# Expert weights in transfers of two chunks: five tiles of 16 KB per partition in a decoder layer on one Trainium2 core

## The chip, the cores and the metric

The kernel runs on one core of a Trainium2 chip. The metric is device time in microseconds (us), the median of three runs. The trace shown here is of one further, profiled execution of the kernel before.

## What is computed

One layer of a decoder on 256 tokens of width 1024 in float32. The last stage is a mixture of experts: each token goes to 2 of 32 experts.

```python
# Layer l:
#   h  = RMSNorm(x)
#   [u | v | q | k | vb] = h @ W_in
#   mixer A: y_a = u * (tril(W_s) RMSNorm(v) + b), chunks of 128
#   mixer B: differential attention with QK-norm and ALiBi
#   merged = sigmoid(h Wg_a) * (y_a Wup_a) + sigmoid(h Wg_b) * (y_b Wup_b)
#   x = x + merged @ W_out
#   x = x + HierMoE(RMSNorm(x))   (top-1 group, then top-2 experts inside the group)
def expert_block(args):
    tk, c = args
    hid = jax.nn.silu(jnp.einsum('td,edf->tef', tk, w1)) * jnp.einsum('td,edf->tef', tk, w3)
    hid = hid * c[:, :, None].astype(hid.dtype)
    return jnp.einsum('tef,efd->td', hid, w2)
```

The experts' weights w1, w3 and w2 are 96 MiB, two thirds of all that the kernel reads.

## The kernel before

**The stream of weights.** All weights reach the core as 136 chunks of 128 partitions x 8 KB (1 MiB): 40 chunks `wf` for the projections, then 96 chunks `wm` for the experts. `Stream` (line 98) sends them in a fixed order on SP's DMA queue. `pump` (line 106) issues the next chunk whenever the number of free slots is above a reserve. The kernel is written with a manual schedule, so the program text sets the order on every queue.

**The slots.** `Slots` (line 50) keeps a list of free buffers. There are 22 slots of 8 KB per partition: 3 are kept for the split projection weights (`hl`), 19 serve everything else: chunks, the activations `xT`, `xh`, `xl`, the mixers' results and so on. Two more are added when early pools close, and the 3 for `hl` join at the end of the projections. In the experts' stage two further slots come from the four-part gate tiles that are no longer needed; a chunk in such a slot is loaded by four transfers of 256 KB, with 2 KB per partition (line 121). A slot that is dropped goes to the end of the list, and `take_chunk` (line 73) takes the first of the list. In the program, the transfer into a slot waits for the last reader of what was there before. The DMA completions of one queue go round eight semaphores (`DMAHW0` to `DMAHW7`), so a transfer also waits until the one eight places before it has landed.

**The experts' stage.** The 32 experts are eight groups of four (`NGRP`). A group (`products`, line 1020) reads 12 chunks. Chunks 0 to 7 hold w1 and w3 for 128 input features each: matmuls of line 1025 into `h`. Then silu and product, two transposes (line 1039), and chunks 8 to 11 hold w2 for 256 output columns each: matmuls of line 1067 into `y`, which line 1046 adds to the tokens' result `res`. In between stand the next group's gathering (line 976). After each chunk `done_` (line 1119) drops the slot and pumps the stream:

```python
        def done_():
            slots.drop(box["w"])
            st.pump(0)
```

Chunk n of the experts is thus chunk n mod 12 of group n div 12. In the last group (`store`), dummy matmuls on a constant (line 215) follow each of the chunks 0 to 7, 20 of them each (30 after the last), and the output columns are copied and stored as soon as they are final.

If a token's expert overflows, a loop repeats the groups; `ci` holds the number of repetitions, 0 with these inputs. Each engine loads it once (line 1145).

Of the kernel before, what the change touches and what calls it, by code (L numbers as in the profile page):

```python
# [5 lines left out]
F32 = mybir.dt.float32  # L6
# [9 lines left out]
P = 128  # L16
# [25 lines left out]
NGRP = 8  # L42
NCH = 12
# [6 lines left out]
class Slots:  # L50


    def __init__(self, pool, tag, n):
        self.free = []
        self.owner = {}
        self.k = 0
        self.add(pool, tag, n)

    def add(self, pool, tag, n):
        self.free += [(pool, f"{tag}{i}") for i in range(n)]  # L60

    def add_pieces(self, pool, tags):
        self.free.append((pool, tags))

    def take(self, shape, dtype, name):
        i = [isinstance(tag, str) for _, tag in self.free].index(True)
        s = self.free.pop(i)
        self.k += 1
        t = s[0].tile(shape, dtype, tag=s[1], name=f"{name}_{self.k}")
# [3 lines left out]
    def take_chunk(self):

        if isinstance(self.free[0][1], str):
            return self.take([P, 2048], F32, "w")
        s = self.free.pop(0)
        self.k += 1
        t = tuple(s[0].tile([P, 512], F32, tag=tag, name=f"w_{self.k}_{i}") for i, tag in enumerate(s[1]))
        self.owner[id(t)] = (s, t)  # L80
        return t

# [15 lines left out]
class Stream:  # L98


    def __init__(self, nc, slots, srcs):
        self.nc, self.slots, self.srcs = nc, slots, srcs
        self.ready = []
        self.i = 0

    def pump(self, reserve):
        while self.i < len(self.srcs) and len(self.slots.free) > reserve:
            src = self.srcs[self.i]
            if self.i == len(self.srcs) - 1:
                if all(not isinstance(tag, str) for _, tag in self.slots.free):  # L110
                    break
                t = self.slots.take([P, 2048], F32, "w")
                c = 0
                for _, w in COLS[-1]:
                    self.nc.sync.dma_start(t[:, c * 8:(c + w) * 8], src[:, c * 8:(c + w) * 8])
                    c += w
            else:
                t = self.slots.take_chunk()
                if isinstance(t, tuple):
                    for e in range(4):  # L120
                        self.nc.sync.dma_start(t[e], src[:, e * 512:(e + 1) * 512])
                else:
                    self.nc.sync.dma_start(t, src)
            self.ready.append(t)
            self.i += 1

    def claim(self):

        t = self.slots.take([P, 2048], F32, "w")
        self.ready.append(t)  # L130
        self.i += 1
        return t
# [16 lines left out]
def body(tc, cp, sp, tp, mmp, axp, xT_d, xn_d, wf_d, wm_d, wst_d, bs_d, pv_d, rb_d, wr_d, out_d):  # L149
    nc = tc.nc  # L150
    V, S, G, TE = nc.vector, nc.scalar, nc.gpsimd, nc.tensor
    slots = Slots(sp, "s", NSLOT - 3)
    hl_slots = Slots(sp, "h", 3)
# [29 lines left out]

    stream = Stream(nc, slots, [wf_d[i] for i in range(40)] + [wm_d[g, c] for g in range(NGRP) for c in range(NCH)])
    pv = cp.tile([P, PV_N], F32, name="pv")
# [960 lines left out]
    with tc.If(more > 0):  # L1146
        with tc.For_i(0, more, 1):
            V.tensor_scalar(pos_m, pos_m, -float(SL), None, ALU.add)
            st = Stream(nc, slots, [wm_d[g, c] for g in range(NGRP) for c in range(NCH)])
            st.pump(0)  # L1150
# [8 lines left out]
def prep(i):  # L1159
# [27 lines left out]
    for _, n in COLS[-1]:  # L1187
# [11 lines left out]
        "wf": wf,  # L1199
        "wm": wm.reshape(NGRP, NCH, P, 2048),  # L1200
        "wst": A("w_s").transpose(2, 0, 1),
# [18 lines left out]
```

## Time and profile before

| quantity | value |
|---|---|
| median of 3 runs | 468.51 us (467.79 to 469.26) |
| profiled execution, its own time | 468.38 us |
| span of the profile | 466.7 us |
| PE busy | 438.9 us (94%) |
| DVE, ACT, POOL busy | 207.4, 175.3, 94.7 us |
| bytes by DMA | 148.80 MB, 319 GB/s over the span |
| transfers of 1 MiB from the experts' weights | 89, and 24 of 256 KB and 2 of 512 KB |

The span is 1.68 us shorter than the execution's own time. PE counts as busy while it runs matmuls, whether they are at full speed or not. The page cuts the span into 40 slices and shows each engine's busy share in tenths, the TensorE clock that was granted, and the GB/s that were moved. The chain of waits follows back from the last instruction what released each step. SP is the engine whose queue issues all weight transfers; a row "SPq" is such an issue.

### The profile page before, as it was taken

The page shows a single profiled execution, that of the slowest core. Times are in us where ns is not written, and L with a number is a line of the kernel's source. Part 1 is how long each engine was busy: PE and PEld are TensorE (multiplying, and loading weights), DVE is VectorE, ACT ScalarE, POOL GpSimd, SP SyncE. Part 2 cuts the span into 40 slices and gives each one's busy share as a digit, 9 for nine tenths or more (in the row PEclk, how much of TensorE's full clock was granted, in tenths as well). Part 3 has the DMA queues.
Part 4 walks back from the last instruction along what each step waited for, and adds up shares of the span by engine and source line. Part 5 has one row for each costly group of instructions (what it writes and reads, how often), then busy time and mean ns, then how long its engine had stood idle before and what let it go on. Part 6 is the DMA issues. An engine that isn't in the chain of part 4 may idle for free.

```text
span 466.7 us, 8463 instructions
## 1 busy us (share of the span) xinstructions
PE 438.9 (94%) x3446; PEld 334.8 (72%) x3446; DVE 207.4 (44%) x389; ACT 175.3 (38%) x332; POOL 94.7 (20%) x118
## 2 busy tenths in 40 slices
PE   8989999999999999999999996989898989889984
PEld 6768778878999999999998842645545554636542
DVE  4676576778797655555774643111111011110012
ACT  5747657665665655533444341111000010101001
POOL 1057296456568100004000100000000000000000
PEclk9999999999999999999999998999999999999998
DMA  7999992550227887598767889999999999999992
GB/s 244 344 425 421 416 402 105 180 179 2 93 91 268 322 312 271 213 364 302 310 239 303 315 326 407 422 418 421 406 418 420 421 418 413 412 421 419 422 382 88
DMA packets 27453, 148.80 MB, mean 319 GB/s; under 512 B 3216, under 2 KB 6032, under 8 KB 11152
## 3 DMA queue, kind: packets, MB, share of 16 engines
q1 hardware_dynamic: 27264, 148.18, 80.3%
q8 instruction: 29, 0.48, 0.4%
q14 instruction: 16, 0.13, 0.1%
q10 hardware_dynamic: 144, 0.02, 0.0%
HBM read 147.14 MB, written 1.05 MB: 318 GB/s over the span
## 4 chain that ended last, share of the span: by engine, by line
PE 81%; DMA 7%; DVE 3%; ACT 3%; issue 2%; POOL 1%; SPq 1%; ACTq 0%
PE h L1025 10%; PE y L1067 7%; PE gp L976 6%; PE res L1046 6%; DMA w<-in_wm_dram 4%; DMA xn<-in_xn_dram 2%; PE v L355 2%; PE u L384 2%; PE ga L386 2%; PE b L386 2%; PE b L385 2%; PE b L384 2%; PE a L386 2%; PE a L385 2%; PE a L384 2%
## 5 line engine op out<-in xcount | busy, mean ns | idle before, releaser
L343 DVE TENSOR_TENSOR hl<-w,hl 128x1024 fp32r<-128x1024 f32 (+2 forms) x88 | 90.8, 1036 | 63.3 <-ACT hl L339 61.0
L339 ACT CAST hl<-w 128x1024 fp32r<-128x1024 f32 (+1 forms) x88 | 84.6, 968 | 83.9 <-PE a L386 12.8
L1025 PE MATMUL h<-w,hT 128*32 128x512 f32 x512 | 61.6, 598 | 0.5 <-DMA w<-in_wm_dram 0.4
L984 DVE TENSOR_TENSOR hT<-gp,pv 128x512 f32<-128x512 f32 (+1 forms) x19 | 11.3, 606 | 98.5 <-PE gp L976 98.5
L345 POOL TENSOR_TENSOR hl<-w,hl 128x352 fp32r<-128x352 f32 x32 | 40.5, 1275 | 21.8 <-ACT hl L339 21.7
L1067 PE MATMUL y<-w,hidT 128*32 128x256 f32 (+1 forms) x528 | 34.1, 389 | 4.9 <-issue 4.4
L1073 ACT COPY yy<-y 128x256 f32<-128x256 f32 (+1 forms) x33 | 12.1, 366 | 69.7 <-PE y L1067 69.7
L976 PEld LDWEIGHTS gp<-Sg,acc 128*128 128x128 f32 x256 | 30.4, 192 | 9.2 <-issue 8.0
L1011 POOL TENSOR_TENSOR Sw<-Sg,C 128x128 f32<-128x128 f32 x16 | 6.1, 399 | 151.4 <-PE res L1046 137.0
L1046 PE MATMUL res<-yy,SwT 128*128 128x128 f32 (+1 forms) x192 | 34.8, 323 | 1.1 <-ACT yy L1073 1.0
L1046 PEld LDWEIGHTS res<-yy,SwT 128*128 128x128 f32 x192 | 25.9, 190 | 12.0 <-issue 6.4
L976 PE MATMUL gp<-Sg,acc 128*128 128x128 f32 x256 | 32.0, 278 | 2.1 <-DVE Sg L972 2.1
L1025 PEld LDWEIGHTS h<-w,hT 128*32 128x32 f32 x512 | 13.4, 109 | 24.6 <-issue 19.2
L1067 PEld LDWEIGHTS y<-w,hidT 128*32 128x32 f32 x528 | 16.1, 112 | 17.1 <-issue 9.7
L1035 ACT ACTIVATE hid<-h 128x256 f32<-128x256 f32 x8 | 3.1, 383 | 54.8 <-PE h L1025 54.8
L1036 DVE TENSOR_TENSOR hid<-hid,h 128x256 f32<-128x256 f32 x8 | 3.4, 421 | 35.1 <-ACT hid L1035 35.1
L215 PEld LDWEIGHTS <-ones_b 128*128 128x128 bf16 x205 | 13.2, 106 | 7.8 <-issue 6.7
L384 PE MATMUL u<-xh,hl 128*128 128x256 f32 x64 | 18.8, 293 | 0.0
L384 PE MATMUL ga<-xh,hl 128*128 128x256 f32 x64 | 18.2, 284 | 0.0
L386 PE MATMUL ga<-xh,hl 128*128 128x256 f32 x64 | 18.1, 283 | 0.0
L385 PE MATMUL ga<-xl,hl 128*128 128x256 f32 x64 | 18.1, 283 | 0.0
L384 PE MATMUL gb<-xh,hl 128*128 128x256 f32 x64 | 18.1, 283 | 0.0
(219 smaller groups left out, 957.3 us busy)
## 6 DMA issues: line engine op xcount, KB each, us to landing
w<-in_wm_dram SPq DMA_DIRECT2D x89, 1024.0 KB, 12.6
w<-in_wf_dram SPq DMA_DIRECT2D x36, 1024.0 KB, 11.6
w<-in_wm_dram SPq DMA_DIRECT2D x24, 256.0 KB, 9.1
w<-in_wf_dram SPq DMA_DIRECT2D x8, 256.0 KB, 4.9
w<-in_wf_dram SPq DMA_DIRECT2D x4, 512.0 KB, 8.2
xT<-in_xT_dram SPq DMA_DIRECT2D x8, 128.0 KB, 4.9
xn<-in_xn_dram SPq DMA_DIRECT2D x1, 1024.0 KB, 8.7
xs<-in_xn_dram SPq DMA_DIRECT2D x1, 1024.0 KB, 9.4
```

The source lines that it names most:

```text
L215: TE.matmul(wps[:, :P], ones_b, ones_b, start=True, stop=True)
L339: S.copy(hl[:, 0, c], raw[:, c])
L343: V.tensor_tensor(hl[:, 1, c.start:m], raw[:, c.start:m], hl[:, 0, c.start:m].bitcast(F32), ALU.subtract)
L345: G.tensor_tensor(hl[:, 1, m:c.stop], raw[:, m:c.stop], hl[:, 0, m:c.stop].bitcast(F32), ALU.subtract)
L384: TE.matmul(o, wh, ah[:, kc], start=kc == 0, stop=False)
L385: TE.matmul(o, wh, al[:, kc], start=False, stop=False)
L386: TE.matmul(o, wl, ah[:, kc], start=False, stop=kc == KC - 1)
L976: TE.matmul(ps[:, i * P:(i + 1) * P], h2[:, t, kc * P:(kc + 1) * P], st["S"][:, t].rearrange("p e s -> p (e s)"), start=start, stop=t == N ...
L1025: TE.matmul(ps[e * SL:(e + 1) * SL], st["h"][kc // 4][:, kc % 4, e * SL:(e + 1) * SL], piece(w, e), start=kc == 0, stop=kc == KC - 1)
L1046: TE.matmul(res[t][c // 512][:, c % 512:c % 512 + n], st["SwT"][:, t * P:(t + 1) * P], yy[:, o:o + n], start=False, stop=True, skip_group_ ...
L1067: TE.matmul(py[e * SL:(e + 1) * SL, :n], hidT[:, f, e * SL:(e + 1) * SL], w[e][:, f], start=f == 0, stop=f == 1)
L1073: S.copy(yy, py[:, :n])
```

## The change

Ten of the 19 slots are now the halves of five tiles of 16 KB per partition, named `sd0` to `sd4`; nine single slots stay. Chunks are ordered on the host so that chunks 2i and 2i+1 of the experts lie side by side, 16 KB per partition. Up to chunk 29 each chunk is loaded alone, into a half or gate parts if one is free, else into a single slot. From chunk 30 to chunk 93 `pump` issues one transfer of 2 MiB for two chunks; it needs a 16 KB tile with both halves free, and stops if there is none. The last two chunks are loaded alone again.

```diff
+NTWO = 5
+TWO = 30
...
-    def __init__(self, pool, tag, n):
+    def __init__(self, pool, tag, n, n2=0):
...
+        for i in range(n2):
+            t = pool.tile([P, 4096], F32, tag=f"{tag}d{i}", name=f"{tag}d{i}")
+            self.free += [("half", t, h) for h in range(2)]
...
+    def pop(self, *kinds):
+
+        for kind in kinds:
+            for s in self.free:
+                if s[0] in kind:
+                    self.free.remove(s)
+                    self.k += 1
+                    return s
+        return None
...
+    def take_two(self):
+
+        for s in self.free:
+            if s[0] == "half":
+                both = [(*s[:2], h) for h in range(2)]
+                if all(any(f[0] == "half" and f[1] is s[1] and f[2] == h for f in self.free) for h in range(2)):
+                    self.free = [f for f in self.free if f[0] != "half" or f[1] is not s[1]]
+                    return s[1], [self.own(x, s[1][:, h * 2048:(h + 1) * 2048]) for h, x in enumerate(both)]
+        return None
...
     def pump(self, reserve):
-        while self.i < len(self.srcs) and len(self.slots.free) > reserve:
+        n = len(self.srcs)
+        while self.i < n and len(self.slots.free) > reserve:
             src = self.srcs[self.i]
-            if self.i == len(self.srcs) - 1:
-                if all(not isinstance(tag, str) for _, tag in self.slots.free):
+            if self.i == n - 1:
+                t = self.slots.take_chunk(("half", "tile"))
+                if t is None:
                     break
...
+            elif self.two <= self.i < n - 2:
+                x = self.slots.take_two()
+                if x is None:
+                    break
+                self.nc.sync.dma_start(x[0], self.pairs[self.i])
+                self.ready += x[1]
+                self.i += 2
+                continue
             else:
-                t = self.slots.take_chunk()
+                t = self.slots.take_chunk(("half", "pieces"), ("tile",))
...
-    slots = Slots(sp, "s", NSLOT - 3)
+    slots = Slots(sp, "s", NSLOT - 3 - 2 * NTWO, NTWO)
...
-    stream = Stream(nc, slots, [wf_d[i] for i in range(40)] + [wm_d[g, c] for g in range(NGRP) for c in range(NCH)])
+    stream = Stream(nc, slots, [wf_d[i] for i in range(40)], wm_d, 40 + TWO)
...
-        "wm": wm.reshape(NGRP, NCH, P, 2048),
+        "wm": wm.reshape(NGRP, NCH // 2, 2, P, 2048).transpose(0, 1, 3, 2, 4).reshape(NGRP, NCH // 2, P, 4096),
```

The instructions of PE, ACT, DVE and POOL keep their order. SP's queue changes at three places. A number at a name's end counts allocations; `sd0_70` and so on are the five wide tiles, and a load of 128x2048 into one of them fills a half.

The first place is SP's queue where chunks 8 to 18 of the experts are loaded, one a row (before the change):

```order
L123 DMA w_63_2295<-in_wm_dram 128x2048 [waits DMAHW0_49,DVE_49]
L123 DMA w_64_2353<-in_wm_dram 128x2048 [waits DMAHW1_49,DVE_49]
L123 DMA w_65_2382<-in_wm_dram 128x2048 [waits DMAHW2_49,PE_49]
L123 DMA w_66_2384<-in_wm_dram 128x2048 [waits DMAHW3_49]
L123 DMA w_67_2415<-in_wm_dram 128x2048 [waits DMAHW4_49,DVE_49]
L123 DMA w_68_2480<-in_wm_dram 128x2048 [waits DMAHW5_49,DVE_49]
L123 DMA w_69_2549<-in_wm_dram 128x2048 [waits DMAHW6_49,DVE_49]
L123 DMA w_70_2618<-in_wm_dram 128x2048 [waits DMAHW7_49,DVE_49]
L123 DMA w_71_2653<-in_wm_dram 128x2048 [waits DMAHW0_49,PE_49]
L123 DMA w_72_2678<-in_wm_dram 128x2048 [waits DMAHW1_49]
L123 DMA w_73_2714<-in_wm_dram 128x2048 [waits DMAHW2_49,DVE_49]
```

and now:

```order
L163 DMA sd0_70<-in_wm_dram 128x2048 [waits DMAHW0_49,DVE_49]
L163 DMA sd0_70<-in_wm_dram 128x2048 [waits DMAHW1_49,DVE_49]
L163 DMA w_65_2345<-in_wm_dram 128x2048 [waits DMAHW2_49,PE_49]
L163 DMA w_66_2347<-in_wm_dram 128x2048 [waits DMAHW3_49]
L163 DMA w_67_2378<-in_wm_dram 128x2048 [waits DMAHW4_49,DVE_49]
L163 DMA sd1_71<-in_wm_dram 128x2048 [waits DMAHW5_49,DVE_49]
L163 DMA w_69_2511<-in_wm_dram 128x2048 [waits DMAHW6_49,DVE_49]
L163 DMA sd1_71<-in_wm_dram 128x2048 [waits DMAHW7_49,DVE_49]
L163 DMA w_71_2614<-in_wm_dram 128x2048 [waits DMAHW0_49,PE_49]
L163 DMA sd2_72<-in_wm_dram 128x2048 [waits DMAHW1_49,DVE_49]
L163 DMA sd2_72<-in_wm_dram 128x2048 [waits DMAHW2_49,DVE_49]
```

Before, each chunk had a slot of its own. Now these chunks lie in the wide tiles: `sd0` holds chunks 8 and 9, `sd1` chunks 13 and 15, `sd2` chunks 17 and 18.

The second place is SP's queue from the load of chunk 25 on. Before:

```order
L123 DMA w_81_2964<-in_wm_dram 128x2048 [waits DMAHW7_49,PE_49]
L123 DMA w_82_2973<-in_wm_dram 128x2048 [waits DMAHW0_49,PE_49]
L123 DMA w_83_2990<-in_wm_dram 128x2048 [waits DMAHW1_49,PE_49]
L123 DMA w_84_3034<-in_wm_dram 128x2048 [waits DMAHW2_49,PE_49]
L123 DMA w_85_3043<-in_wm_dram 128x2048 [waits DMAHW3_49,PE_49]
L123 DMA w_86_3052<-in_wm_dram 128x2048 [waits DMAHW4_49,PE_49]
L123 DMA w_87_3069<-in_wm_dram 128x2048 [waits DMAHW5_49,PE_49]
L123 DMA w_88_3080<-in_wm_dram 128x2048 [waits DMAHW6_49,PE_49]
L123 DMA w_89_3099<-in_wm_dram 128x2048 [waits DMAHW7_49,PE_49]
L123 DMA w_90_3112<-in_wm_dram 128x2048 [waits DMAHW0_49,PE_49]
```

and now:

```order
L163 DMA sd3_73<-in_wm_dram 128x2048 [waits DMAHW7_49,PE_49]
L163 DMA sd3_73<-in_wm_dram 128x2048 [waits DMAHW0_49,PE_49]
L163 DMA sd4_74<-in_wm_dram 128x2048 [waits DMAHW1_49,PE_49]
L163 DMA w_84_2990<-in_wm_dram 128x2048 [waits DMAHW2_49,PE_49]
L163 DMA w_85_2999<-in_wm_dram 128x2048 [waits DMAHW3_49,PE_49]
L1185 TENSOR_LOAD ci_2867 [waits DVE_49]
L1185 ISA x2
L153 DMA sd0_70<-in_wm_dram 128x4096 [waits DMAHW4_49,PE_49]
L153 DMA sd1_71<-in_wm_dram 128x4096 [waits DMAHW5_49,PE_49]
L153 DMA sd2_72<-in_wm_dram 128x4096 [waits DMAHW6_49,PE_49]
L153 DMA sd3_73<-in_wm_dram 128x4096 [waits DMAHW7_49,DMAHW0_49,PE_49]
L153 DMA sd4_74<-in_wm_dram 128x4096 [waits DMAHW1_49,PE_49]
```

Chunks 25, 26 and 27 now lie in `sd3`, `sd3` and `sd4`; the other half of `sd4` holds chunk 5. From chunk 30 on one transfer of 4096 elements per partition stands for two of 2048. Before, the sixth row (chunk 30) took the slot of chunk 5; now the first wide transfer goes to `sd0`, so it waits for PE to be done with chunks 8 and 9. The load of the repetition count has moved from the queue's end to a place ahead of the wide transfers.

The third place is the end of the stream on SP's queue. Before:

```order
L123 DMA w_147_3868<-in_wm_dram 128x2048 [waits DMAHW5_49,PE_49]
L123 DMA w_148_3874<-in_wm_dram 128x2048 [waits DMAHW6_49,PE_49]
L123 DMA w_149_3893<-in_wm_dram 128x2048 [waits DMAHW7_49,PE_49]
L123 DMA w_150_3906<-in_wm_dram 128x2048 [waits DMAHW0_49,PE_49]
L115 DMA w_151_3932<-in_wm_dram 128x1024 [waits DMAHW1_49,PE_49]
L115 DMA w_151_3932<-in_wm_dram 128x1024 [waits DMAHW2_49]
```

and now:

```order
L153 DMA sd4_74<-in_wm_dram 128x4096 [waits DMAHW4_49,PE_49]
L153 DMA sd0_70<-in_wm_dram 128x4096 [waits DMAHW5_49,PE_49]
L153 DMA sd1_71<-in_wm_dram 128x4096 [waits DMAHW6_49,PE_49]
L161 DMA w_86_0_3912<-in_wm_dram 128x512
L161 DMA w_86_1_3913<-in_wm_dram 128x512
L161 DMA w_86_2_3914<-in_wm_dram 128x512
L161 DMA w_86_3_3915<-in_wm_dram 128x512 [waits DMAHW7_49]
L147 DMA w_87_3920<-in_wm_dram 128x1024 [waits DMAHW0_49]
L147 DMA w_87_3920<-in_wm_dram 128x1024 [waits DMAHW1_49]
```

The wide transfers are 32, and each takes the tile that the one five places before it filled. Chunk 94 goes into gate parts and chunk 95 into a single slot, whose readers have long been done, so that only the tiles are waited for.

## Rows read from the trace of the kernel before

**Rows 1.** Page, busy time by engine and the 40 slices of GB/s.

```profile
PE 438.9 (94%) x3446; PEld 334.8 (72%) x3446; DVE 207.4 (44%) x389; ACT 175.3 (38%) x332; POOL 94.7 (20%) x118
...
GB/s 244 344 425 421 416 402 105 180 179 2 93 91 268 322 312 271 213 364 302 310 239 303 315 326 407 422 418 421 406 418 420 421 418 413 412 421 419 422 382 88
```

**Rows 2.** Windows: start:end length, busy by engine, PE clock, DMA share, GB/s.

```profile
280.00:290.00 10.00, 5.75 (x48) 2.73 (x44) 3.85 (x15) 2.32 (x6) 0.48 (x2) 0.96 0.99 404
290.00:300.00 10.00, 10.00 (x97) 6.43 (x94) 1.19 (x3) 1.49 (x4) 0.76 (x2) 0.87 1.01 423
310.00:320.00 10.00, 8.35 (x94) 5.40 (x90) 1.54 (x3) 1.50 (x4) 0.76 (x2) 1.00 1.02 424
```

**Rows 3.** Waits of SP's queue, 340 to 440 us: total, times, longest.

```profile
SPq L123 <- DMA w<-in_wm_dram: 63.1, 35, 3.0
...
SPq L123 <- PE h L1025: 0.4, 2, 0.2
```

**Rows 4.** Waits of PE's weight loads, 290 to 430 us.

```profile
PEld h L1025 <- DMA w<-in_wm_dram: 2.1, 7, 0.3
```

**Rows 5.** Timeline of PE, last group: start, us, line, operation, [idle before <- releaser].

```profile
430.17 1.06 PE L1025 MATMUL h<-w,hT 128*32 128x512 f32 x8
...
432.38 1.06 PE L1025 MATMUL h<-w,hT 128*32 128x512 f32 x8
...
446.64 1.07 PE L1025 MATMUL h<-w,hT 128*32 128x512 f32 x8 [0.19 <-DMA w<-in_wm_dram]
...
450.28 1.07 PE L1067 MATMUL y<-w,hidT 128*32 128x256 f32 x16 [0.56 <-issue]
...
458.22 0.65 PE L1067 MATMUL y<-w,hidT 128*32 128x128 f32 x16
```

**Rows 6.** Timeline of SP's queue, three narrow windows around single issues.

```profile
293.17 0.33 SPq L123 DMA_DIRECT2D w<-in_wm_dram  x1
...
305.12 0.59 SPq L123 DMA_DIRECT2D w<-in_wm_dram  x1
...
309.82 0.33 SPq L123 DMA_DIRECT2D w<-in_wm_dram  x1
```

**Rows 7.** Timeline of PE in groups 0 to 2.

```profile
289.85 3.25 PE L1067 MATMUL y<-w,hidT 128*32 128x256 f32 x32 [0.52 <-DVE hidT L1041]
...
303.14 3.64 PE L1025 MATMUL h<-w,hT 128*32 128x512 f32 x32
...
312.70 1.93 PE L1067 MATMUL y<-w,hidT 128*32 128x256 f32 x32 [0.63 <-issue]
...
322.46 1.92 PE L1025 MATMUL h<-w,hT 128*32 128x512 f32 x16
...
324.68 3.64 PE L1025 MATMUL h<-w,hT 128*32 128x512 f32 x32
...
344.00 1.49 PE L1025 MATMUL h<-w,hT 128*32 128x512 f32 x12
```

**Rows 8.** Transfers of `w`, issue to landing, window 180 to 256 us.

```profile
DMA to landing us min/median/max: 4.7/6.7/10.1
```

**Rows 9.** DMA: packets and mean rate, 410 to 430 us, then 393.2 to 394.8 us.

```profile
DMA packets 1153, 8.41 MB, mean 421 GB/s; under 512 B 127, under 2 KB 127, under 8 KB 127
...
q1 hardware_dynamic: 1151, 8.39, 101.0%
...
DMA packets 176, 0.68 MB, mean 425 GB/s; under 512 B 21, under 2 KB 21, under 8 KB 117
...
q1 hardware_dynamic: 176, 0.68, 107.1%
```

**Rows 10.** Timeline of DVE: the repetition count.

```profile
282.32 0.15 DVE L1139 CAST ci<-cs 128x1 int32<-128x1 f32 x1
```

**Rows 11.** Page, the two queues that load instructions: packets, MB, share of 16 engines.

```profile
q8 instruction: 29, 0.48, 0.4%
q14 instruction: 16, 0.13, 0.1%
```

More of the change, by code (lines that the diff above doesn't have):

```diff
@@ L57, in __init__ @@
         self.add(pool, tag, n)
+        for i in range(n2):
+            t = pool.tile([P, 4096], F32, tag=f"{tag}d{i}", name=f"{tag}d{i}")
+            self.free += [("half", t, h) for h in range(2)]
     def add(self, pool, tag, n):
-        self.free += [(pool, f"{tag}{i}") for i in range(n)]
+        self.free += [("tile", pool, f"{tag}{i}") for i in range(n)]
     def add_pieces(self, pool, tags):
[L63 to L69, printed above, removed]
+        self.free.append(("pieces", pool, tags))
@@ L70, in take, with own @@
+    def pop(self, *kinds):
[6 more added lines that the diff above has]
+        return None
+    def own(self, s, t):
         self.owner[id(t)] = (s, t)
         return t
[L73 to L81, printed above, removed]
+    def take(self, shape, dtype, name):
+        s = self.pop(("tile",))
+        return self.own(s, s[1].tile(shape, dtype, tag=s[2], name=f"{name}_{self.k}"))
@@ new lines, in take_chunk @@
+    def take_chunk(self, *kinds):
+        s = self.pop(*kinds)
+        if s is None:
+            return None
+        if s[0] == "half":
+            t = s[1][:, s[2] * 2048:(s[2] + 1) * 2048]
+        elif s[0] == "tile":
+            t = s[1].tile([P, 2048], F32, tag=s[2], name=f"w_{self.k}")
+        else:
+            t = tuple(s[1].tile([P, 512], F32, tag=tag, name=f"w_{self.k}_{i}") for i, tag in enumerate(s[2]))
+        return self.own(s, t)
+    def take_two(self):
+        for s in self.free:
+            if s[0] == "half":
+                both = [(*s[:2], h) for h in range(2)]
+                if all(any(f[0] == "half" and f[1] is s[1] and f[2] == h for f in self.free) for h in range(2)):
+                    self.free = [f for f in self.free if f[0] != "half" or f[1] is not s[1]]
+                    return s[1], [self.own(x, s[1][:, h * 2048:(h + 1) * 2048]) for h, x in enumerate(both)]
+        return None
@@ L98, with __init__ @@
 class Stream:
-    def __init__(self, nc, slots, srcs):
-        self.nc, self.slots, self.srcs = nc, slots, srcs
+    def __init__(self, nc, slots, wf, wm, two):
+        self.nc, self.slots, self.two = nc, slots, two
+        self.srcs = wf + [wm[g, c // 2][:, c % 2 * 2048:(c % 2 + 1) * 2048] for g in range(NGRP) for c in range(NCH)]
+        self.pairs = [None] * len(wf) + [wm[g, c // 2] for g in range(NGRP) for c in range(NCH)]
         self.ready = []
@@ L106, in pump @@
     def pump(self, reserve):
-        while self.i < len(self.srcs) and len(self.slots.free) > reserve:
+        n = len(self.srcs)
+        while self.i < n and len(self.slots.free) > reserve:
             src = self.srcs[self.i]
-            if self.i == len(self.srcs) - 1:
-                if all(not isinstance(tag, str) for _, tag in self.slots.free):
+            if self.i == n - 1:
+                t = self.slots.take_chunk(("half", "tile"))
+                if t is None:
                     break
-                t = self.slots.take([P, 2048], F32, "w")
                 c = 0
@@ L127, in claim @@
     def claim(self):
-        t = self.slots.take([P, 2048], F32, "w")
+        t = self.slots.take_chunk(("half",))
         self.ready.append(t)
@@ L1148, in body @@
             V.tensor_scalar(pos_m, pos_m, -float(SL), None, ALU.add)
-            st = Stream(nc, slots, [wm_d[g, c] for g in range(NGRP) for c in range(NCH)])
+            st = Stream(nc, slots, [], wm_d, 0)
             st.pump(0)
```

## The prediction

> **What bounds the kernel now.** I read the page first. PE is busy 94% of the span, but the bytes moved stand at 406 to 422 GB/s in each slice from the 25th to the 38th, that is from about 280 us to 443 us [rows 1]. So there are two candidates for the experts' stage, and the reader should look at who waits for whom.
>
> The queue that issues the weights waits, from 340 to 440 us, 63.1 us for earlier transfers to land and 0.4 us for matmuls of line 1025 to free a slot [rows 3]. So the stream is never short of slots there: the transfers stand back to back and the rate of the DMA engines sets their pace. PE, on its side, waits only 2.1 us for weights from 290 to 430 us [rows 4]: it lives on chunks that were loaded ahead. One group starts at 322.46 and the next at 344.00 [rows 7], 21.54 us for 12 chunks or 1.80 us per chunk, while a chunk takes the DMA 1.0486 MB / 421 GB/s = 2.49 us [rows 9]. The lead is eaten up, and it is just used up at the end: in the last group PE waits for chunk 91, and its matmuls start at 446.64 [rows 5]. After that the kernel ends by a chain of matmuls, copies and stores that no longer waits for weights. So before the change the prefetched lead carries PE through to the last group, and **the lead exists because slots free one by one and are refilled at once.** That is what I follow through the change.
>
> **The change, part by part.**
>
> *Order.* From chunk 30 on, single slots are not used any more; only five tiles of two chunks are. Pair 0 (chunks 30 and 31) goes to the tile of chunks 8 and 9, pair 1 to that of chunks 13 and 15, pair 2 to that of 17 and 18, pair 3 to that of 25 and 26, pair 4 to that of 5 and 27; pair j takes the tile of pair j-5 after that. A transfer into a tile waits for PE to be done with the later of its two chunks. Before, chunk 30 waited for chunk 5.
>
> *When PE is done with these chunks.* Until PE runs short of weights it keeps its times. Chunks 8 and 9 are the 32 matmuls that start at 289.85 and last 3.25 us [rows 7]; the issue at 293.17 in the trace is the transfer that waits for them [rows 6]. In the same way 305.12 is the issue that waits for chunk 15 and 309.82 the one for chunk 18 [rows 6]. Chunk 26 is the first of the four chunks that start at 324.68 and take 3.64 us [rows 7]; chunk 15 is the second of the same run a group earlier, released 1.98 us after that run's start at 303.14, so chunk 26 is released about 0.9 us sooner after its run's start, at 324.68 + 1.1 = 325.8.
>
> *Time of a wide transfer.* No 16 KB row of weights is in the trace, so this is bounded. With no gain it is two chunks, 2.097 MB / 421 GB/s = 4.98 us. For the gain I solve two windows for a fixed time per packet. From 410 to 430 us 1151 packets with 8.39 MB took 101.0% of 16 engines for 20 us, 323.2 us; from 393.2 to 394.8 us, with the 2 KB rows of the gate parts, 176 packets with 0.68 MB took 107.1% of 16 engines for 1.6 us, 27.4 us [rows 9]. Two equations give an estimate of 15 ns per packet. A wide transfer saves 9 packets per engine (8 rows and one completion), 0.13 us: **4.86 us per pair.** The ends kept for the range are 4.98 (nothing saved) and 4.72 (twice as much). I take 4.86, which lies between them and comes from rows of the same queue. What surrounds a transfer, from issue to landing, is 4.7 us in the quickest case [rows 8], less 2.49 us of transfer: 2.2 us.
>
> A rule speaks for the change here. The Trainium skill, "DMA: Bandwidth & Descriptors", section "Anatomy of one DMA", gives each transfer a fixed time of about 2 us beside its bytes, and its rules for kernel authors ask for large transfers. By that rule the pairs would save some 2 us each and the weights would cease to be the bound, which gives the time of the second rival. This case's trace disagrees where transfers are queued: a MB-sized one lands every 2.49 us with all of its bytes accounted for by the rate, so the fixed time lies beside other transfers.
>
> *The stream now.* Pair 0 lands at 293.17 + 2.2 + 4.86 = 300.2. Pair 1 is issued at 305.12 and lands at 312.2: the DMA engines stand idle for about 7 us. Pair 2, issued at 309.82, follows at once and lands at 317.0. Pair 3 is issued at 325.8 and lands at 332.9: some 11 us idle. A third, smaller hole lies ahead of pair 0. From pair 3 on the stream closes up: pair 4's tile is free at 326.7; pair 5 needs chunks 30 and 31, done by 330.23 + 1.9 = 332.2, and starts later than that; pair 7 needs the last chunks of group 2, done before the next group starts at 344.00 [rows 7], and starts at 347.5. Later on four pairs, 19 us, are always queued, more than PE needs for one. So pair 30 (chunks 90 and 91) lands at 332.9 + 27 x 4.86 = **464.1**. In the trace of before chunk 91 was there at 446.45, since PE waited 0.19 us and started at 446.64 [rows 5]. Chunk 37, 54 chunks earlier, was then there about 54 x 2.49 = 134.5 us before that, at 312; now it lands at 332.9. So 21 us are lost in the holes, and about 3 us come back by faster rows and by one load in gate parts less often.
>
> *The end.* PE needs 21.54 / 6 = 3.59 us per pair and the stream 4.86, so PE's lead of 344.0 - 332.9 = 11.1 us at the start of group 3 is gone after some 9 pairs, near 376 us; from there PE follows the stream. In the last group a chunk costs PE 2.21 us with its dummy matmuls (430.17 to 432.38 [rows 5]), 4.42 us per pair, still under 4.86. Chunks 90 and 91 now arrive together: chunk 90's matmuls start at 464.1, chunk 91's 2.21 us later at 466.3. From there to the first matmul of line 1067 it is 450.28 - 446.64 = 3.64 us [rows 5]: 469.95. Pair 31 has landed at 469.0, and chunks 94 and 95 (5 us more of DMA, 474.0) are needed only at about 475 and 478: before, the last matmuls of line 1067 stand at 458.22, 7.94 us behind the first [rows 5]. So the whole end moves by 469.95 - 450.28 = 19.7 us.
>
> *At no cost.* Fewer issues on SP: SP waits for landings or PE anyway. The load of `ci`, now ahead of pair 0 on SP: DVE writes its value at 282.32 [rows 10], and SP waits until 293.17 for pair 0. If the value came later than that, pair 0 would be late by as much. In the projections the chunks go into other slots, but the queue order is the same and loading runs ahead of its use; if that cover were gone PE would show waits for `w` before 270 us.
>
> **Sum.** The profiled execution took 468.38 us (span 466.7), 0.13 us under the median of 468.51, which needs no correction. 468.38 + 19.7 = **488.0 us**, 4% slower.
>
> **The rivals.**
>
> *A. The clock falls and PE becomes the bound.* In the trace, after a stretch with PE busy 5.75 of 10 us, the granted clock is 0.96 and then 0.87 over 10 us, a stay at 1.2 GHz of some us, and two chunks of line 1067 take 3.25 us where at 2.4 GHz they take 1.93 [rows 2, 7]. With 8.35 of 10 us busy it stayed at 1.00 [rows 2]. In the new stream PE works 21.5 of 29.2 us, between the two. If the clock stayed at half from pair 12 on, a pair would cost PE 7.2 us instead of the stream's 4.86; over the 18 pairs to pair 30 that is 42 us more, 530 us. Against it: at half clock PE would not wait, and the clock came back in the trace as soon as PE was busy. The Trainium skill, "TensorE: Matmul & The Clock Gate", section "HAM oscillation", tells of just this, a kernel that waits for transfers and starts each piece of work at the low clock; the trace agrees that the clock falls after a stretch of waits, and does not show it staying low. Single drops cost 1.3 us each and vanish in the 1.3 us per pair that PE has to spare, except in the last group, where up to 3 us may come through.
>
> *B. Not slower: wide transfers move so much faster that the stream is no bound.* PE alone, never waiting, would reach chunk 91 at 430.17 + 7 x 2.21 + 0.4 = 446.0 instead of 446.64: 467.8 us, no measurable change, and this is the floor for any DMA speed. It decides where pair 30 lands by 443.8: (443.8 - 332.9) / 27 = 4.11 us per pair, 510 GB/s. No window of the trace reaches more than 425.
>
> *C. 16 KB rows are slower than two of 8 KB.* The instruction queue q8 moves 16 KB packets: 0.4% of 16 engines for 466.7 us is 29.9 us for 29 packets, 1.03 us each. Such rows would make a pair 8.2 us and, over 28 pairs, the time 582 us. But q14's 8 KB packets take 7.5 us / 16 = 0.47 us by the same account [rows 11], against some 0.31 us for those of weights (323.2 us for 1024 [rows 9]): both wait for their turn on busy engines, and 16 KB costs about twice 8 KB.
>
> That the change does not do what it says is excluded: the program's queue holds the 32 wide transfers.
>
> **How the numbers follow.** The forecast has 0.90, A 0.04, B 0.03, C 0.03. With 4.72 us per pair the forecast's time is 484.1, with 4.98 us 491.4, and with drops of the clock in the last group up to 494.5: the range is 484 to 494.5 and leaves out A, B and C. A measurement of this kernel can tell about 0.3% (1.4 us) from no change. B splits into 0.02 for the same and 0.01 for faster; all else is slower.
>
> **What the profile after would show.** Slices with less than 300 GB/s between 287 and 328 us, then some 430 GB/s to about 470; SP's queue waiting for PE (line of `h` and `y`) around 293, 305 and 326 us; PE's waits for `w` from about 376 us on, some 8 us per group; the last matmul of line 1067 (now 1107) near 478 us. Wrong would be: a rate above 480 GB/s (B), PE clock under 0.9 from 380 us on with SP waiting for PE (A), under 400 GB/s in a full stream (C), or wide transfers issued before 293 us, which would mean that I took the wrong chunks for the tiles.

## The result, and the profile after

The changed kernel takes 488.67 us (median of 4 runs, 486.60 to 490.02), the kernel before beside it 468.65 (467.79 to 469.26): a ratio of 1.042, 95% interval 1.038 to 1.046. The profiled execution is the slowest of the four, 490.02 us with a span of 488.2.

The page of the changed kernel, busy time, clock and rate by slice, against [rows 1]:

```profile
PE 448.6 (92%) x3446; PEld 338.6 (69%) x3446; DVE 207.1 (42%) x389; ACT 175.3 (36%) x332; POOL 92.8 (19%) x118
...
PEclk9999999999999999999999989999998987988999
...
GB/s 247 346 424 422 377 200 125 174 136 149 95 215 294 352 268 193 368 305 342 218 294 362 290 215 173 342 94 434 428 422 427 427 430 427 426 430 426 426 373 94
```

PE's share hardly falls, from 94 to 92%; a reader of the shares alone would find nothing. The row of rates has it: 215, 173, 342 and 94 GB/s in the slices from 281 to 329 us, where before 406 and more stood, and then 422 to 434 up to 464 us. Windows of the same stretch show the holes closer (columns as in [rows 2]):

```profile
290.00:300.00 10.00, 9.48 (x104) 6.63 (x103) 1.61 (x4) 1.49 (x4) 0.76 (x2) 1.00 0.58 211
300.00:310.00 10.00, 10.00 (x87) 4.13 (x85) 0.69 (x1) 0.37 (x1) 0.00 (x0) 1.00 0.45 159
310.00:320.00 10.00, 8.35 (x95) 5.48 (x91) 1.54 (x3) 1.50 (x4) 0.76 (x2) 1.00 0.65 264
320.00:330.00 10.00, 10.00 (x90) 5.41 (x90) 0.65 (x3) 0.75 (x2) 0.00 (x0) 1.00 0.35 131
330.00:340.00 10.00, 8.35 (x89) 5.11 (x82) 2.07 (x4) 1.50 (x4) 0.76 (x2) 1.00 1.01 431
```

From 290 to 330 us 7.65 MB were moved; at 421 GB/s [rows 9] it would have been 16.84. The 9.19 MB that are missing are 21.8 us of transfers, about what the kernel became slower by. PE is as busy there as before: it pays later. The smaller hole ahead of pair 0 adds some more: 284 GB/s from 280 to 290 us, where it was 404 [rows 2].

The first four issues of pairs on SP's queue, from four narrow windows of its timeline, against [rows 6], and ahead of them the matmuls of chunks 8 and 9, which end at 292.60 and which pair 0 waited for:

```profile
290.67 1.93 PE L1107 MATMUL y<-sd,hidT 128*32 128x256 f32 x32 [0.52 <-DVE hidT L1081]
...
292.67 0.33 SPq L153 DMA_DIRECT2D sd<-in_wm_dram  x1
...
304.63 0.33 SPq L153 DMA_DIRECT2D sd<-in_wm_dram  x1
...
309.33 0.33 SPq L153 DMA_DIRECT2D sd<-in_wm_dram  x1
...
325.31 1.19 SPq L153 DMA_DIRECT2D sd<-in_wm_dram  x2
```

The tile `sd` over the same stretch, from issue to landing, and what SP's queue waited for from 290 to 330 us, which answers to [rows 3] for this stage:

```profile
DMA to landing us min/median/max: 7.5/7.7/11.7
...
SPq L153 <- PE h L1065: 31.9, 4, 15.6
SPq L153 <- PE y L1107: 10.0, 1, 10.0
```

Through all of this stretch SP's queue waits for PE to give tiles back, and for no landing at all. The transfer into an idle queue lands 7.5 to 7.7 us after its issue; pair 3 so lands at 325.31 + 7.7 = 333.0.

From there the stream is full. Packets from 410 to 430 us, against [rows 9], and PE's waits for weights from 300 to 480 us:

```profile
DMA packets 591, 8.54 MB, mean 427 GB/s; under 512 B 69, under 2 KB 69, under 8 KB 69
...
q1 hardware_dynamic: 589, 8.52, 100.4%
...
PE h L1065 <- DMA sd<-in_wm_dram: 12.7, 6, 3.0
...
PE y L1107 <- DMA sd<-in_wm_dram: 3.4, 3, 1.4
```

Half as many packets carry the same bytes 1.4% faster: 2.097 MB / 427 GB/s = 4.91 us per pair. PE's timeline where it meets the stream, against [rows 5, 7]:

```profile
368.47 1.92 PE L1065 MATMUL h<-sd,hT 128*32 128x512 f32 x16 [1.13 <-DMA sd<-in_wm_dram]
...
442.20 2.99 PE L1107 MATMUL y<-sd,hidT 128*32 128x256 f32 x32 [1.02 <-DMA sd<-in_wm_dram]
...
453.60 1.06 PE L1065 MATMUL h<-sd,hT 128*32 128x512 f32 x8
...
467.13 1.07 PE L1065 MATMUL h<-sd,hT 128*32 128x512 f32 x8
...
469.35 1.06 PE L1065 MATMUL h<-sd,hT 128*32 128x512 f32 x8
...
472.99 1.07 PE L1107 MATMUL y<-sd,hidT 128*32 128x256 f32 x16 [0.56 <-DVE hidT L1081]
...
480.93 0.65 PE L1107 MATMUL y<-w,hidT 128*32 128x128 f32 x16
```

PE first waits for weights at 368.47. At 442.20 it still waits for pair 25. In the last group (453.60 on) it waits for none: chunks 90 and 91 start at 467.13 and 469.35, at PE's own pace of 2.22 us. Whether PE or the stream set the end there is what one experiment below asks.

### The profile page after: what moved, and what is told of

The parts are those of the page before. It is cut to its first block, busy times and chain, and to the rows that moved or that the text cites. A ratio compares the mean times of both kernels' runs of the same rounds, so it can differ in the third digit from the quotient of the medians.

```text
span 488.2 us, 8365 instructions
## 1 busy us (share of the span) xinstructions
PE 448.6 (92%) x3446; PEld 338.6 (69%) x3446; DVE 207.1 (42%) x389; ACT 175.3 (36%) x332; POOL 92.8 (19%) x118
## 4 chain that ended last, share of the span: by engine, by line
PE 72%; DMA 20%; DVE 2%; ACT 2%; issue 1%; SPq 1%; ACTq 0%
DMA sd<-in_wm_dram 13%; PE y L1107 7%; PE h L1065 7%; PE res L1086 6%; PE gp L1016 5%; DMA sd<-in_wf_dram 5%; DMA wsb<-in_bs_dram 3%; PE wps L255 2%; PE v L395 2%; PE u L424 2%; PE ga L426 2%; PE b L426 2%; PE b L425 2%; PE b L424 2%; PE a L426 2%; PE a L425 2%
## 5 line engine op out<-in xcount | busy, mean ns | idle before, releaser
L383 DVE TENSOR_TENSOR hl<-sd,hl 128x1024 fp32r<-128x1024 f32 (+2 forms) x80 | 81.0, 1016 | 54.1 <-ACT hl L379 53.5
L379 ACT CAST hl<-sd 128x1024 fp32r<-128x1024 f32 (+1 forms) x80 | 76.2, 960 | 71.0 <-PE a L426 9.1
L1065 PE MATMUL h<-sd,hT 128*32 128x512 f32 x424 | 56.7, 642 | 12.7 <-DMA sd<-in_wm_dram 12.7
L385 POOL TENSOR_TENSOR hl<-sd,hl 128x352 fp32r<-128x352 f32 x32 | 40.6, 1278 | 21.8 <-ACT hl L379 21.2
L1016 PE MATMUL gp<-Sg,acc 128*128 128x128 f32 x256 | 34.7, 293 | 2.1 <-DVE Sg L1012 2.1
L1065 PEld LDWEIGHTS h<-sd,hT 128*32 128x32 f32 x424 | 11.2, 112 | 36.0 <-DMA sd<-in_wm_dram 16.9
L1107 PE MATMUL y<-sd,hidT 128*32 128x256 f32 x384 | 27.0, 414 | 5.9 <-DMA sd<-in_wm_dram 3.4
L1107 PEld LDWEIGHTS y<-sd,hidT 128*32 128x32 f32 x384 | 12.6, 116 | 15.4 <-issue 9.9
L424 PE MATMUL gb<-xh,hl 128*128 128x256 f32 x64 | 18.1, 283 | 0.0
L425 PE MATMUL gb<-xl,hl 128*128 128x256 f32 x64 | 18.1, 283 | 0.0
L426 PE MATMUL gb<-xh,hl 128*128 128x256 f32 x64 | 18.1, 283 | 0.0
```

Of the source, the lines that this page charges most:

```text
L379: S.copy(hl[:, 0, c], raw[:, c])
L383: V.tensor_tensor(hl[:, 1, c.start:m], raw[:, c.start:m], hl[:, 0, c.start:m].bitcast(F32), ALU.subtract)
L385: G.tensor_tensor(hl[:, 1, m:c.stop], raw[:, m:c.stop], hl[:, 0, m:c.stop].bitcast(F32), ALU.subtract)
L424: TE.matmul(o, wh, ah[:, kc], start=kc == 0, stop=False)
L425: TE.matmul(o, wh, al[:, kc], start=False, stop=False)
L426: TE.matmul(o, wl, ah[:, kc], start=False, stop=kc == KC - 1)
```

## The experiments

The theory: the time is lost because too little can be loaded ahead. Between pair 0 and the end of chunks 30 and 31 there are places for only ten chunks, while the single slots that come free stay empty; the stream stands still, and PE's lead is gone. The rivals: the wide transfer with its 16 KB rows costs the time; the new tiles, the weights' layout or the later loads in the projections do; or it is the pairing, the wait for the later of two chunks.

**No pairs at all.**

```
-TWO = 30
+TWO = 200
```

> The five 16 KB tiles, the weights' layout in DRAM (rows of two chunks side by side) and the order of slots stay; only no chunk is ever loaded as a pair (the switch to pairs is set behind the last chunk), so all slots are used to the end. Theory (holes: from pair 0 to the end of chunk 31 only ten chunks have a place): the holes go and the time is that of the kernel before, 468.5 us, between 467 and 470. Rival (the tiles, the layout with rows 16 KB apart or the later loads in the projections cost the time): about 488.7 us, as with pairs.

Measured: 468.67 us (10 runs), ratio 1.001 (0.999 to 1.003). Two windows of its trace:

```profile
300.00:310.00 10.00, 8.98 (x76) 3.62 (x68) 1.11 (x2) 0.76 (x2) 0.00 (x0) 1.00 1.01 420
...
320.00:330.00 10.00, 10.00 (x87) 4.10 (x85) 0.69 (x1) 0.37 (x1) 0.00 (x0) 1.00 1.02 412
```

The holes are gone (159 and 131 GB/s with pairs). Tiles, layout and the order of slots up to chunk 29 cost nothing that can be measured: the 20 us come from what is done from chunk 30 on, the pairs and the single slots left empty.

**Pairs, but two transfers each.**

```
-                self.nc.sync.dma_start(x[0], self.pairs[self.i])
+                for h in range(2):
+                    self.nc.sync.dma_start(x[1][h], self.srcs[self.i + h])
```

> The rule of the pairs stays (a tile is filled only when both halves are free), but two transfers of 1 MiB with 8 KB rows take the place of one of 2 MiB with 16 KB rows. Theory (holes): SP's issues stand at 293, 305, 309 and 325 us as with pairs, the holes stay, and a pair takes 2 x 2.49 = 4.98 us where it took 4.91: over 28 pairs 2 us more, less what chunk 90 gains by landing ahead of chunk 91; 487 to 492 us. Rival (the wide transfer or its 16 KB rows are what costs): 468.5 us.

Measured: 491.27 us (4 runs), ratio 1.051 (1.047 to 1.056). Its packets from 410 to 430 us:

```profile
DMA packets 1153, 8.41 MB, mean 420 GB/s; under 512 B 128, under 2 KB 128, under 8 KB 128
...
q1 hardware_dynamic: 1152, 8.39, 100.8%
```

The wide transfer is not what costs. It is worth 427 instead of 420 GB/s, 4.91 against 4.99 us per pair or 2.3 us over 28 pairs; the runs differ by 2.6, and their ratios, 1.038 to 1.046 and 1.047 to 1.056, just fail to overlap. The run changes a little more than the size: in its trace the two transfers of pair 1 go out apart, at 302.02 and 304.24 us, each when its own half is free, where the wide one went out at 304.63. This also measures the rule weighed in the prediction, of the Trainium skill, "DMA: Bandwidth & Descriptors", section "Anatomy of one DMA" (some 2 us beside the bytes of each transfer, which the section gives for another issue path than SP's): here, in a full queue, one transfer more per pair costs 0.08 us. Where a pair is alone the trace agrees with the rule: 7.5 us from issue to landing for 4.91 us of bytes.

**Ten places, each refilled alone.** This one parts "too few places" from "waiting for the later of two".

```
-                x = self.slots.take_two()
-                if x is None:
+                t = self.slots.take_chunk(("half",))
+                if t is None:
                     break
-                self.nc.sync.dma_start(x[0], self.pairs[self.i])
...
+                self.nc.sync.dma_start(t, src)
```

> From chunk 30 on chunks go only into the ten halves, as with pairs, but each is loaded alone, as soon as its own half is free; single slots still stay empty. This parts two readings of the holes. Theory (too few places): chunk 40 must wait for chunk 30 to be used, so between about 293 and 331 us only ten chunks, 25 us of transfers, can be loaded, and some 13 to 15 us are still lost; 483 to 489 us. Rival (waiting for the later of two chunks is what opens the holes): the halves are refilled one by one, the holes close, 468 to 473 us.

Measured: 487.90 us (4 runs), ratio 1.042 (1.038 to 1.046). The same four windows:

```profile
290.00:300.00 10.00, 8.09 (x72) 5.10 (x73) 1.54 (x3) 1.97 (x5) 0.76 (x2) 0.83 0.53 188
300.00:310.00 10.00, 10.00 (x90) 4.70 (x90) 0.49 (x2) 0.76 (x3) 0.00 (x0) 1.00 0.48 176
310.00:320.00 10.00, 8.35 (x83) 5.57 (x81) 1.54 (x3) 1.13 (x3) 0.76 (x2) 1.00 0.82 306
320.00:330.00 10.00, 10.00 (x100) 4.88 (x102) 1.19 (x3) 1.12 (x3) 0.00 (x0) 1.00 0.19 55
```

Each half is refilled by itself, and the holes are there all the same: 7.25 MB in 40 us, against 7.65 with pairs. So the number of places is the main cause, with 19 of the 20 us. That the pairing as such costs nothing is not shown. The nearest comparison is the run above with two transfers per pair, which also moves 1 MiB at a time: it took 3.4 us longer (491.27), and the ratios of the two just fail to overlap. With pairs the half that chunk 5 leaves stays empty until chunk 27 is used; here it is refilled at 281.78 us, so one chunk more, 2.49 us of transfer, is loaded ahead. The rule by pairs may thus cost some 3 us, about what the faster wide rows give back; four runs of each do not settle its size.

**Four tiles instead of five.**

```
-NTWO = 5
+NTWO = 4
```

> As with pairs, but only four of the 16 KB tiles and two single slots more (which stay empty from chunk 30 on too). Theory (too few places): between pair 0 and the end of chunk 31 there is room for eight chunks instead of ten, so one transfer of 4.91 us fewer fits into that stretch, all of it is lost at the end: 488.7 + 4.9 = 493.6 us, between 492 and 495.5. Rival (the holes come from which chunks share a tile, not from the number of tiles): 487 to 490 us.

Measured: 494.26 us (4 runs), ratio 1.053 (1.048 to 1.058). The window in which the missing tile's pair was loaded, and the first issue of a pair:

```profile
290.00:300.00 10.00, 9.42 (x100) 6.49 (x101) 1.62 (x5) 1.49 (x4) 0.76 (x2) 1.00 0.01 2
...
304.98 0.33 SPq L153 DMA_DIRECT2D sd<-in_wm_dram  x1
```

One pair of places less makes one transfer less fit ahead, here the first one, and the end moves by 5.6 us where 4.9 were expected from the transfer. The dose answers to the theory.

**Pairs where a tile is free, else one chunk in a single slot or gate parts.** A half whose neighbour is still in use stays empty here too.

```
-                x = self.slots.take_two()
-                if x is None:
-                    break
+                x = self.slots.take_two() if self.i % 2 == 0 else None
...
+                t = self.slots.take_chunk(("tile",), ("pieces",))
```

> A pair is loaded by one transfer when some tile has both halves free; if none has, one chunk is loaded alone into any free slot. The program then holds 12 wide transfers instead of 32, and no slot stays empty. Theory (holes): no holes, 467 to 470 us. Rival (wide transfers cost): 12/32 of the 20.2 us lost come back as a cost, about 476 us.

Measured: 471.15 us (10 runs), ratio 1.009 (1.006 to 1.012): 17.5 of the 20 us come back, though not all, and the time lies just above the theory's 467 to 470. Part of what is left can be read in the last group (chunks 90 and 91; this profiled execution took 469.19 us, one of the fastest of the ten):

```profile
446.01 1.06 PE L1072 MATMUL h<-sd,hT 128*32 128x512 f32 x8 [1.13 <-DMA sd<-in_wm_dram]
...
448.23 1.07 PE L1072 MATMUL h<-sd,hT 128*32 128x512 f32 x8
```

Here the two are a pair. Chunk 90 waits 1.13 us for it, and chunk 91 starts 1.6 us later than before, 448.23 against 446.64 [rows 5]. The prediction has this cost of the coarser grain at the end of its chain; my expectation for this run left it out.

**The same, with fewer dummy matmuls in the last group,** looking for a version with wide transfers that beats the kernel before.

```
-NW = (20, 10)
+NW = (12, 10)
```

> A pair where a tile has both halves free, else one chunk in any free slot (as in the earlier run of this kind, 471.2 us), and 12 instead of 20 dummy matmuls in the last group. Sought is a version that uses wide transfers and still beats the kernel before. Theory (stream and PE meet in the last group): 12 wide transfers save 12 x 0.07 = 0.8 us of the stream, the fewer dummies 0.5 us to 2 us: 468 to 470.5 us, no better than the kernel before. Rival (the last group is PE's): 466 to 468 us.

Measured: 471.16 us (12 runs), ratio 1.006 (1.003 to 1.009), above both expectations: a miss. Chunk 90 now waits still longer for its pair:

```profile
446.91 1.10 PE L1072 MATMUL h<-sd,hT 128*32 128x512 f32 x8 [3.07 <-DMA sd<-in_wm_dram]
...
449.34 1.94 PE L1072 MATMUL h<-sd,hT 128*32 128x512 f32 x8
```

PE is done sooner, waits 3.07 us, and chunk 91 then takes 1.94 us where 1.07 is usual; from 449 to 452 us the granted clock is 0.63, so part of that stretch is at 1.2 GHz. Nothing is gained.

**The same again, but singly from chunk 82 on.**

```
-                x = self.slots.take_two() if self.i % 2 == 0 else None
+                x = self.slots.take_two() if self.i % 2 == 0 and self.i < n - 14 else None
```

> A pair where a tile has both halves free, else one chunk in any free slot, but from chunk 82 on one chunk at a time; 12 instead of 20 dummy matmuls in the last group. The program holds 10 wide transfers. Set against the two earlier runs with pairs up to the last group (471.2 us both). Theory (a pair that lands as one makes chunk 90 wait for chunk 91, which costs half a pair, 2.5 us, in the last group alone): 466 to 468.5 us. Rival (the wide transfers or holes earlier in the stream made those two slower): 470 to 472 us.

Measured: 469.05 us (12 runs), ratio 1.002 (0.999 to 1.005), between the two expectations and nearer to the theory. The grain at the end accounts for a part of the excess; the interval of the run before it overlaps, and what the rest is stays open. A hole of about 1.3 us is left in its trace between 290 and 300 us, where the DMA share is 0.87:

```profile
290.00:300.00 10.00, 10.00 (x101) 6.64 (x94) 1.18 (x3) 1.49 (x4) 0.76 (x2) 0.89 0.87 344
```

**The clock kept up.** Nine dummy matmuls behind each of the first eight chunks of groups 3 to 6, which add work and change no output.

```
...
                 if store:
                     warm(NW[0])
+                elif g >= 3 and final_pass:
+                    warm(9)
...
```

> As with pairs, with nine dummy matmuls (0.06 us each) behind each of the first eight chunks of groups 3 to 6, which before had none; nothing else is changed. They take 0.55 us per chunk and fit into the 1.3 us per pair that PE waits. Theory (the half-clock spells after waits made the last group start late, at 453.60 us in the profile with pairs, though its weights were there): the granted clock stays at 1.00 from 330 us on, PE waits for the weights of chunk 90 in the last group, whose pair lands at 325.3 + 2.2 + 28 x 4.91 = 465.0, the first matmul of line 1107 starts at 465.0 + 2.2 + 3.6 = 470.8 instead of 472.99, and the time is 486 to 488 us, its runs within 1.5 us of each other. Rival (the stream's end alone sets the time, and the spells cost nothing): 488.7 us, with the same spread as before, 3 us.

Measured: 490.93 us (6 runs), ratio 1.047 (1.043 to 1.051). A miss: 2.3 us more than with pairs alone, where 1 to 3 us less were expected, and above the rival's 488.7 too. A window and three rows of PE's timeline:

```profile
440.00:460.00 20.00, 17.68 (x181) 11.12 (x182) 1.25 (x3) 1.86 (x5) 0.76 (x2) 0.91 1.01 428
...
442.75 3.29 PE L1109 MATMUL y<-sd,hidT 128*32 128x256 f32 x32 [2.13 <-DMA sd<-in_wm_dram]
...
453.86 1.07 PE L1065 MATMUL h<-sd,hT 128*32 128x512 f32 x8
...
473.26 1.07 PE L1109 MATMUL y<-sd,hidT 128*32 128x256 f32 x16 [0.56 <-issue]
```

The granted clock is 1.00 in the windows from 290 to 440 us, where it was 0.78 and 0.91 with pairs, and nothing is gained: PE is ready for pair 25 at 440.62 instead of 441.18 us and waits 2.13 instead of 1.02 for it. Pair 25 landed at 420.05 + 22.6 = 442.65 us there, 6.3 us behind pair 24, where 4.9 is usual, though pair 3 had gone out 0.86 us earlier (324.45); what delayed it is open. The one spell at 1.2 GHz that remains, behind the wait for pair 25, is the one that the pairs' own profile also has there (2.99 us at 442.20, where the 32 matmuls take 1.93 at 2.4 GHz [rows 7]). So no time is to be had from the spells in the middle. That they cost nothing at all is not shown, as the dummy matmuls take time of PE themselves.

**Fewer dummy matmuls in the last group, with pairs.**

```
-NW = (20, 10)
+NW = (12, 10)
```

> As with pairs, with 12 instead of 20 dummy matmuls behind each of the first eight chunks of the last group. It asks what sets the end there. In the profile with pairs the last group starts at 453.60 us and goes through its chunks every 2.21 us without a wait. Theory (it starts some 3 us behind the stream, because the rest of group 6 stands between, and with 2 x 2.21 = 4.42 us per pair gains only 0.49 us per pair on it, so PE's own pace sets the end): with 1.72 us per chunk PE waits for the last pairs, chunk 90 lands at 465.0, chunk 91 starts at 466.7 and not at 469.35; 485 to 487 us. Rival (the landing of the last pair sets the end, as I had predicted): only the dummies behind chunk 91 go, 0.5 us, 488 to 489 us.

Measured: 486.83 us (6 runs), ratio 1.041 (1.037 to 1.045). The time lies where the theory put it, but the trace speaks for the rival. SP's issue of pair 3, and PE's timeline:

```profile
323.98 1.19 SPq L153 DMA_DIRECT2D sd<-in_wm_dram  x2
...
440.62 3.06 PE L1107 MATMUL y<-sd,hidT 128*32 128x256 f32 x32 [1.01 <-DMA sd<-in_wm_dram]
...
465.19 1.06 PE L1065 MATMUL h<-sd,hT 128*32 128x512 f32 x8 [1.29 <-DMA sd<-in_wm_dram]
...
466.96 1.07 PE L1065 MATMUL h<-sd,hT 128*32 128x512 f32 x8
...
470.21 1.07 PE L1107 MATMUL y<-sd,hidT 128*32 128x256 f32 x16 [0.63 <-DMA sd<-in_wm_dram]
```

PE now waits for pair 30, which makes its landing visible: five pairs after pair 25, 24.57 us or 4.91 each. Put into the pairs' own profile, where pair 25 had landed by the chain at 421.98 + 20.09 = 442.07, pair 30 was there at 466.64, and PE took it up at 467.13. That execution's own rows agree: pair 30 went out at 445.23 and landed 21.3 us later, at 466.53. PE was only 0.5 to 0.6 us behind the stream, and not the 2 to 3 us of my theory, which had put that landing at 465.0. Of the profile's 2.78 us to the first matmul of line 1107 (470.21 against 472.99), 1.3 to 1.6 are an earlier start of the whole stream (pair 3's issue 1.33 and pair 25's matmuls 1.58 us earlier), which the edit cannot have brought, and the rest, 1.2 to 1.5 us, goes with the dummy matmuls.

**Fewer dummy matmuls in the kernel before,** at 12 and then 6 per chunk; the edit is to the kernel before the change.

```
-NW = (20, 10)
+NW = (12, 10)
```

> The kernel before, with 12 instead of 20 dummy matmuls behind each of the first eight chunks of the last group. It shows how near PE's own pace in the last group was to being the bound there. Theory (the stream lands chunk 91 at 446.45 us and PE would be there at 446.0): PE waits for weights earlier in the group and gains only what follows chunk 91, 8 x 0.06 = 0.5 us: 467.0 to 468.5 us. Rival (PE's pace was the bound): 8 x 8 x 0.06 = 3.9 us less, 464 to 465 us.

Measured: 466.71 us (12 runs) against 468.75 for the kernel before beside it (23 runs), ratio 0.995 (0.993 to 0.998). It beats both kernels, by little, and lies just below the theory's range. PE's timeline, chunks 88 and 91 and the first of line 1067:

```profile
437.39 1.06 PE L1025 MATMUL h<-w,hT 128*32 128x512 f32 x8 [0.65 <-DMA w<-in_wm_dram]
...
444.85 1.06 PE L1025 MATMUL h<-w,hT 128*32 128x512 f32 x8 [0.65 <-DMA w<-in_wm_dram]
...
447.99 1.07 PE L1067 MATMUL y<-w,hidT 128*32 128x256 f32 x16 [0.52 <-DVE hidT L1041]
```

PE waits 0.63 to 0.65 us for each of the last four chunks: the stream sets the pace there, 7.46 us from the first to the last of them or 2.49 per chunk, as in [rows 9]. From chunk 91 to line 1067 it takes 3.14 instead of 3.64 us, the 0.5 expected. The median gains 2.0; where the other 1.5 us come from these runs don't settle.

```
-NW = (20, 10)
+NW = (6, 10)
```

> The kernel before with 6 instead of 20 dummy matmuls per chunk in the last group (12 gave 466.7 us against 468.7). Theory (with 12 PE already waits 0.65 us for each of the last chunks, so the stream sets the end, and only what stands behind chunk 91 gets shorter, 6 x 0.06 = 0.4 us): 466 to 467 us. Rival (with PE idle for half of the last group its clock falls, and the chain behind chunk 91 runs at 1.2 GHz): 468 to 472 us.

Measured: 466.77 us (12 runs), ratio 0.999 (0.996 to 1.002). The median is that of 12 dummies, but the comparison finds no difference from the kernel before. Fewer than 12 buy nothing that can be measured, and the rival's fall to 468 to 472 us is not seen.

## Why the prediction was right

*The bound and the order.* Pairs 0 to 3 were forecast for 293.17, 305.12, 309.82 and 325.8 us and went out at 292.67, 304.63, 309.33 and 325.31: the right chunks for each tile, each 0.5 us early. (Pair 0 so went out just ahead of the 293 us named as a sign of wrong chunks, but behind the matmuls of the right ones, which ended at 292.60.) Landings: 300.2, 312.1, 318.6 and 333.0, against 300.2, 312.2, 317.0 and 332.9 forecast. That three of them agree to 0.1 us is luck: a pair alone took 7.5 to 7.7 us to land, where 2.2 + 4.86 = 7.06 were forecast, and the early issues made up for it. The holes are where they were put.

*How the holes were explained.* The prediction had two reasons in one sentence, that slots free one by one and that they are refilled at once. The runs part them: with ten halves refilled one by one nearly the whole loss is still there (487.90 us), while the number of places moves the time (four tiles 494.26, all slots 468.67). Refilling by pairs adds perhaps some 3 us to that.

*The time per pair* is the term that was mis-sized. I took 4.86 us, from an estimate of 15 ns per packet; the full stream shows 4.91, and from pair 3's landing to pair 30's it is (466.64 - 333.0) / 27 = 4.95, inside the ends 4.72 to 4.98 and near the upper one. That is 2.4 us. The estimate's wide rows were to gain 0.12 us per pair over 4.98; in the full stream they gained 0.07 to 0.08. Over the first pairs a landing came later than the rate alone says: pair 4 at 326.17 + 11.7 = 337.9, pair 5 at 331.72 + 11.8 = 343.5, 5.6 us apart, by the issues and landings of `sd`. What delayed it is open.

*The end.* I had the first matmul of line 1107 at 469.95; it came at 472.99. The 3.0 us are 0.1 for pair 3, 2.4 for the pairs, 0.5 by which PE took up chunk 90 late. The steps behind it held: 2.22 us from chunk 90 to 91 (2.21 forecast), 3.64 from there to line 1107 (3.64), 7.94 to its last matmuls (7.94, at 480.93; 478 forecast).

*The sum* came to 488.0 and the profiled execution to 490.02: 3.0 us more up to line 1107, 1.2 less behind it (from the last matmuls of that line to the end of the span 7.27 us, before 8.48, for a reason that is open), 0.14 more outside the span. The four runs lie from 486.60 to 490.02; that their median, 488.67, is only 0.7 us from the sum is in part luck, as the steps of the profiled execution add up to 2 us more.

*PE's lead* was to be gone near 376 us; the first wait is at 368.47. The mean of 3.59 us per pair hid that PE takes a group's first eight chunks faster than the rest. It moved no other number, as PE waits for the stream from then on either way. Its waits are 5.4 us per group on PE (16.1 us from 300 to 480, all in groups 4 to 6), not 8, and the last group has none: part of the slack went into the spells at 1.2 GHz.

*The rivals.* The clock did fall (A), to 0.78 from 400 to 420 us, and SP did wait for PE, 70.6 us from 340 to 440 against 25.6 for landings (before, 0.4 for line 1025 against 63.1 [rows 3]). So both signs that the prediction gave for A were there from 400 to 420 us, and A was still not the case. The window, two of SP's waits, and the time from issue to landing of `sd` from 400 to 420 us:

```profile
400.00:420.00 20.00, 15.71 (x123) 7.91 (x120) 2.23 (x4) 1.21 (x4) 0.76 (x2) 0.78 1.01 427
...
SPq L153 <- PE h L1065: 29.9, 12, 3.4
...
SPq L153 <- DMA sd<-in_wm_dram: 25.6, 15, 2.5
...
DMA to landing us min/median/max: 21.1/21.4/22.4
```

With 21 us from issue to landing four pairs are queued, so SP can wait for PE while the queue stays full: 427 GB/s, and PE waits for weights. It is the rate of the queue and PE's waits for weights that tell A from the forecast. Each spell ended by itself, and holding the clock up gained nothing. The Trainium skill, "TensorE: Matmul & The Clock Gate", section "HAM oscillation", describes waits for transfers that leave the next piece of work at the low clock. The trace agrees in part: behind the wait of 2.98 us at 432.32 the 16 matmuls take 3.33 us, behind one of 1.13 us at 368.47 they take 1.92. Holding the clock up won back nothing of the loss that the section counts. In the last group it may count: there chunk 91 took 1.94 us behind a wait of 3.07, in the run with pairs or single chunks and 12 dummies. B and C fell with 427 GB/s.

*At no cost.* The projections loaded later (377 and 200 GB/s in the fifth and sixth slices, 416 and 402 before [rows 1]) without a loss, as the run without pairs shows. The load of `ci` held nothing up: pair 0 went out half a microsecond early.

## What to carry to other kernels

Before two small transfers are made into one large one, count what can still be loaded ahead: a buffer that may only be refilled whole, or is left unused, takes prefetch depth away, and in a kernel that lives on a lead this costs about the time that the queue stands empty, less what faster transfers win back (here 20 us lost in all, with some 2.3 won back). Look for the cost in the rate of the DMA queue by slice, not in the share of the busy engine, which moved from 94 to 92%. What the issuing queue waits for tells the reason, but only where the rate falls: from 340 to 440 us it waited 70.6 us for PE with the queue full. Where a stream sets the end, try small last pieces, since the last but one waits for the last when they land as one (here chunk 90 waited 1.13 and 3.07 us; what that is worth in time is not settled).

## What the runs showed of the hardware beyond this

A spell at 1.2 GHz in the stage that runs on its lead seems to delay the start of the stream. In the pairs' profile one lies in the window from 280 to 290 us (granted clock 0.83); in the profiles with pairs and 12 dummies and with the clock kept up there is none (1.00). Pair 3 was issued at 325.31, 323.98 and 324.45 us. Whether such a delay reaches the end is not shown: pair 25's matmuls stood at 442.20, 440.62 and 442.75, so the third profile had lost its gain by then. No run here forced such a spell.
